# A mixture-of-experts decoder layer on one core: one pair of experts combined per turn, single buffers, four more weight tiles filled early, six PSUM banks in one rotation, and the last down weights in a half and two quarters

## The chip, the core and the metric

The kernel runs on one core of a Trainium2 chip. It is one program: TensorE (PE) multiplies, VectorE (DVE) and ScalarE (ACT) read the products out of PSUM, GpSimd (POOL) fetches rows of tokens by index, and SyncE (SP) issues the transfers of the weights from HBM, which the core's 16 DMA engines carry out. The metric is the device time of one execution in microseconds (us). Three runs of the kernel before took 767.46, 767.82 and 767.86 us, with a median of 767.82 us.

## The reference: what is computed

One decoder layer on 512 tokens of width 1024. The first part is a shared norm, an input projection, a short gated convolution, differential attention and an output projection. The second part is a mixture of 32 experts (4 groups of 8): each token picks the best group and its two best experts in it.

```python
hn2 = rms_norm(h, ffn_norm_g[l]).reshape(Bsz * S, D)
# hierarchical_moe, S = 512 tokens, D = 1024, D_EXPERT = 512:
p_group = softmax(hn2 @ w_router_group);  g_idx = argmax(p_group);  g_gate = max(p_group)
logits_sel = (hn2 @ w_router_expert) of the chosen group
top_vals, top_idx = lax.top_k(logits_sel, 2);  top_w = softmax(top_vals)
comb = onehot(g_idx) * (sum of onehot(top_idx) * top_w) * g_gate
for g in range(G):
    hg = jnp.einsum('td,edf->tef', h, w_gate[g])
    hu = jnp.einsum('td,edf->tef', h, w_up[g])
    act = jax.nn.silu(hg) * hu * comb[:, g, :, None]
    y = y + jnp.einsum('tef,efd->td', act, w_down[g])
```

All inputs are float32. Each expert has three matrices of 2 MB (gate, up, down), so the 32 experts hold 192 MB of weights, and every one of them is read once.

## The kernel before

The first part (to line 650) runs projection, convolution, attention and the first half of the output projection. From line 692 the second half of the output projection, the router and the places of the tokens in the experts are computed (lines 840 to 862).

The second part takes the experts in 16 pairs. Each expert has 64 slots for tokens, so a pair fills 128 partitions. A weight matrix is cut into pieces of 1 MB: four pieces for gate and up of an expert, two for down, 192 pieces in all. The list `pieces` (lines 703 to 709) is the order in which SP issues them: gate and up of expert 2q, the four down pieces of pair q-1, gate and up of expert 2q+1. A piece goes into a tile; there are 17 of them, the 16 tiles of `ring` (named `we`) and one tile `wm` in the pool `moe` (line 728). Before the router twelve pieces are issued (`pump(RING - 4)`, line 737), after it five more (line 866), because the last four tiles of `ring` and the space of `moe` are still used by the first part. From there `used(n)` (line 1119) counts tiles that PE has read, and SP issues one new piece into each.

A turn q of the loop at line 1146 does, in this order on PE:
- `expert(2q)`: gate and up (`gate_up`, lines 966 and 967, tile `pgu`), two matmuls side by side in the two halves of the array. ACT applies silu into its own tile `sil` (line 972) and DVE multiplies into `act` (line 973).
- `down_t(q-1)`: the activations of the pair before are transposed (`pat2`, line 979) and copied to SBUF by ACT (`aT`, line 981).
- `turned(q+1)`: the rows of the next pair (`xr`) are transposed (`pxt2`, line 953) and scaled into `xt` by ACT (line 959) and DVE (line 956).
- `down_pair(q-1)`: the down matmuls (`pdn`, line 990), whose result is split into a rounded part `rh` (ACT, line 1007) and a rest `rl` (DVE, line 1008). `sel` (line 1018) holds a one for each token and slot that belong together.
- `expert(2q+1)`.
- In even turns the indices and the rows of two pairs are made ready (`prepare`, lines 934 to 944; POOL fetches `xr` at line 925 and the gates `cw` at line 930), and `combine_all` adds two pairs into the output `y`: eight times four matmuls into one bank (`pcb`, lines 1026 and 1027) and one addition by DVE (line 1030).

The tiles `xr`, `xt`, `act`, `rh`, `rl` and `sel` have two buffers each. The eight PSUM banks are two each for `G` (pgu), `A` (pat2, pxt2, pi), `D` (pdn) and `C` (pcb), at line 1111.

After the loop (lines 1164 to 1176) pair 14 is combined, the activations of pair 15 are transposed, its down matmuls run in two halves of 512 columns (`down_cols`, line 999), each half is split and combined, and the output leaves in eight transfers (line 1175). `overflow` (line 1054) reads a count (`tot`) into a register of each engine and loops over experts with more than 64 tokens; the count itself is computed by DVE in turn 1 (`overflow_count`, lines 1035 to 1047).

The order on each engine is the order of the code (`manual_schedule`); the waits between engines are put in from the tiles that they share.

Of the kernel before, what the change touches and what calls it, by code (L numbers as in the profile page):

```python
# [17 lines left out]
P = 128  # L18
D = 1024
S = 512  # L20
# [12 lines left out]
MORE = 1  # L33
# [6 lines left out]
def layer(ctx: ExitStack, tc: tile.TileContext, x, attn_norm_g, w_in, conv_w, conv_out_g,  # L40
# [653 lines left out]
    ws_cm.__exit__(None, None, None)  # L694
    kp = ctx.enter_context(tc.tile_pool(name="kp", bufs=1, side="right", reuse_waits="tile"))
# [17 lines left out]
    def w_src(e, j):  # L713
# [6 lines left out]
        if isinstance(e, int) and e >= NE - 2:  # L720
            return src[:, :, 512 * (j - 4):512 * (j - 4) + 512], (4, 512)
        return src[:, 2 * (j - 4):2 * (j - 4) + 2], (2, 1024)

    def load_piece(e, j):
        src, shape = w_src(e, j)
        i = slot[0] % (RING + MORE)
        slot[0] += 1
        t = rtile("we", [P, *shape]) if i < RING else moe.tile([P, *shape], F32, name="wm", tag=f"wm{i}")
        nc.sync.dma_start(t, src)
        return t  # L730
# [6 lines left out]
    pump(RING - 4)  # L737
# [157 lines left out]
    HS = (slice(0, SLOTS), slice(SLOTS, P))  # L895
    vcol = kp.tile([P, PAIRS], F32, name="vcol")
    tokrow = kp.tile([P, S], F32, name="tokrow")
# [20 lines left out]
    def fetch(i, m):  # L918
        x = moe.tile([P, D], F32, name="xr", tag="xr", bufs=2)
# [14 lines left out]
    def prepare(qs, tag="A"):  # L934

        n = len(qs)
        oh = one_hot(posm[:, :, 2 * qs[0]:2 * qs[0] + 2 * n], 2 * n)

        def rest():
            ix = [index(oh[:, :, P * j:P * (j + 1)], vcol[:, q:q + 1], tag) for j, q in enumerate(qs)]  # L940
            for q, i in zip(qs, ix):
                rows[q], cws[q] = fetch(i, P)
            return lambda: [fetch_gates(cws[q], i, P) for q, i in zip(qs, ix)]
        return rest

    def turned(x, m, tag="A"):

        xt = moe.tile([P, KD, P], F32, name="xt", tag="xt", bufs=2)
# [260 lines left out]
```

## Time and profile before

| | |
|---|---|
| median of three runs | 767.82 us |
| profiled execution, its own time | 767.56 us |
| its span in the trace | 765.8 us |
| mean granted TensorE clock | 0.975 of full speed |
| busy: PE, PE weight loads, DVE, ACT, POOL | 690.6, 379.6, 300.9, 192.4, 76.4 us |
| moved by DMA | 229.68 MB |
| weights of the experts | 192 transfers of 1024 KB |

The profile's own time is 1.8 us longer than the span, which counts from the first instruction to the last. The busy time of PE holds the modelled ends of pipelined matmuls that overlap, two side by side in the expert part, so it does not say that PE is the limit. Stage by stage the profile has to be read with the share of the DMA engines and the rate beside it: the first 220 us have little DMA, and from about 290 us on to 730 us the DMA engines are busy all the time.

### The profile page before, as it was taken

To read this page: it belongs to the slowest core of one execution; us is meant where nothing else is said; L and a number is where in the kernel's file an instruction comes from. 1 tells how busy PE (TensorE), PEld (TensorE's weight loads), DVE (VectorE), ACT (ScalarE), POOL (GpSimd) and SP (SyncE) were. 2 spreads that over 40 slices of the span, in tenths; PEclk is the share of its full clock that TensorE was granted. 3 is DMA by queue.
4 is the path that set the end of the run, shared out by engine and by line. 5 is a ranking of instruction groups with operands and counts; after the bars stand their busy time and mean duration, and the time that the engine had idled before them with its cause. 6 is when DMAs were issued, how large, how long until landed. Compare 5 with 4: busy or idle time off the path is not lost.

```text
span 765.8 us, 8682 instructions
## 1 busy us (share of the span) xinstructions
PE 690.6 (90%) x3272; PEld 379.6 (50%) x3272; DVE 300.9 (39%) x593; ACT 192.4 (25%) x413; POOL 76.4 (10%) x103
## 2 busy tenths in 40 slices
PE   6998999999899659999999999989989988998984
PEld 5886788777778423334335344334334334333331
DVE  2565866777551722143224134124123223113232
ACT  3555445555341211110211021111010210110100
POOL 5021301121010122002002002002002002000001
PEclk9999999999999859999999999999999999999997
DMA  8221222211159959999999999999999999999942
GB/s 260 85 83 55 83 58 72 64 56 56 56 180 422 384 184 415 417 422 416 421 422 415 422 421 416 422 420 416 422 419 417 422 420 419 419 422 422 408 156 110
DMA packets 54842, 229.68 MB, mean 300 GB/s; under 512 B 6303, under 2 KB 20912, under 8 KB 30736
## 3 DMA queue, kind: packets, MB, share of 16 engines
q1 hardware_dynamic: 50384, 222.32, 72.4%
q0 software_dynamic: 3312, 4.64, 2.0%
q10 hardware_dynamic: 1104, 2.17, 0.7%
q8 instruction: 26, 0.43, 0.2%
q14 instruction: 16, 0.13, 0.0%
HBM read 229.16 MB, written 4.26 MB: 305 GB/s over the span
## 4 chain that ended last, share of the span: by engine, by line
PE 52%; DMA 29%; DVE 9%; ACT 5%; issue 2%; POOL 1%; SPq 0%; DVEq 0%; POOLq 0%; ACTq 0%
DMA we<-in_w_exp_up_dram 18%; PE pgu L966 13%; PE pdn L990 7%; DMA we<-in_w_exp_down_dram 6%; PE pgu L967 4%; DMA wm<-in_w_exp_down_dram 3%; PE pq L118 3%; PE pq L119 3%; PE pq L117 3%; PE pcb L1026 2%; DMA xr<-hrow,idx 2%; PE pcb L1027 2%; PE pcv L117 1%; PE pcv L119 1%; PE pcv L118 1%
## 5 line engine op out<-in xcount | busy, mean ns | idle before, releaser
L967 PE MATMUL pgu<-we,xt 128*64 128x512 f32 x488 | 218.4, 599 | 13.7 <-DMA we<-in_w_exp_up_dram 13.7
L966 PE MATMUL pgu<-we,xt 128*64 128x512 f32 x480 | 215.1, 599 | 0.8 <-ACT xt L959 0.8
L973 DVE SCALAR_TENSOR_TENSOR act<-sil,cw,pgu 64x512 f32<-64x512 f32 x32 | 36.0, 1126 | 222.7 <-ACT sil L972 222.7
L990 PE MATMUL pdn<-we,aT 128*64 128x512 f32 x448 | 109.4, 598 | 0.8 <-ACT aT L981 0.8
L966 PEld LDWEIGHTS pgu<-we,xt 128*64 128x64 f32 x480 | 64.4, 138 | 90.3 <-issue 85.9
L967 PEld LDWEIGHTS pgu<-we,xt 128*64 128x64 f32 x488 | 65.3, 138 | 64.2 <-issue 37.2
L972 ACT ACTIVATE sil<-pgu,cw 64x512 f32<-64x512 f32 x32 | 21.9, 683 | 289.5 <-PE pgu L967 264.7
L990 PEld LDWEIGHTS pdn<-we,aT 128*64 128x64 f32 x448 | 35.1, 138 | 58.9 <-issue 54.5
L1026 PE MATMUL pcb<-rh,sel 128*128 128x512 f32 x128 | 55.1, 430 | 9.0 <-DVE y L1030 9.0
L1008 DVE TENSOR_TENSOR rl<-pdn,rh 128x512 fp32r<-128x512 f32 x32 | 22.1, 692 | 89.9 <-ACT rh L1007 89.9
L1030 DVE TENSOR_TENSOR y<-y,pcb 128x512 f32<-128x512 f32 x70 | 47.1, 687 | 21.8 <-PE pcb L1027 21.5
L1027 PE MATMUL pcb<-rl,sel 128*128 128x512 f32 x128 | 51.1, 400 | 0.6 <-DVE rl L1008 0.6
L925 POOL DMA_INDIRECT xr<-hrow,idx x16 | 16.1, 1004 | 344.3 <-DVE vcol L915 332.5
L109 DVE TENSOR_TENSOR wlo<-raw,whi 128x1024 fp32r<-128x1024 f32 x30 | 37.7, 1255 | 22.7 <-ACT whi L102 22.7
L1007 ACT ACTIVATE rh<-pdn 128x512 fp32r<-128x512 f32 x32 | 19.1, 597 | 100.4 <-PE pdn L990 96.6
L117 PE MATMUL pq<-whi,xh 128*128 128x512 f32 x96 | 40.9, 427 | 2.5 <-DVE st0h L356 1.6
L117 PE MATMUL pcv<-xh,whi 128*128 128x512 f32 x96 | 41.8, 435 | 0.0
L118 PE MATMUL pq<-wlo,xh 128*128 128x512 f32 x96 | 38.9, 405 | 0.5 <-DVE wlo L109 0.5
L119 PE MATMUL pq<-whi,xl 128*128 128x512 f32 x96 | 39.1, 407 | 0.0
L119 PE MATMUL pcv<-xh,wlo 128*128 128x512 f32 x96 | 38.1, 397 | 0.0
L1026 PEld LDWEIGHTS pcb<-rh,sel 128*128 128x128 f32 x128 | 24.4, 191 | 27.5 <-DVE y L1030 20.3
L118 PE MATMUL pcv<-xl,whi 128*128 128x512 f32 x96 | 37.9, 395 | 0.0
(233 smaller groups left out, 923.5 us busy)
## 6 DMA issues: line engine op xcount, KB each, us to landing
we<-in_w_exp_up_dram SPq DMA_DIRECT2D x61, 1024.0 KB, 19.8
we<-in_w_exp_gate_dram SPq DMA_DIRECT2D x60, 1024.0 KB, 19.8
we<-in_w_exp_down_dram SPq DMA_DIRECT2D x60, 1024.0 KB, 19.8
raw<-in_w_in_dram SPq DMA_DIRECT2D x24, 512.0 KB, 3.7
raw<-in_w_out_dram SPq DMA_DIRECT2D x8, 512.0 KB, 3.9
wm<-in_w_exp_gate_dram SPq DMA_DIRECT2D x4, 1024.0 KB, 19.8
wm<-in_w_exp_down_dram SPq DMA_DIRECT2D x4, 1024.0 KB, 19.8
wm<-in_w_exp_up_dram SPq DMA_DIRECT2D x3, 1024.0 KB, 19.8
```

The source lines that it names most:

```text
L109: V.tensor_sub(los[i], raws.pop(i), his[i].bitcast(F32))
L117: T.matmul(o, lh, rh, start=start, stop=False)
L118: T.matmul(o, lh, rl, start=False, stop=False)
L119: T.matmul(o, ll, rh, start=False, stop=stop)
L966: T.matmul(p[HS[1 - h]], l, w[2 * (k // 4)][:, k % 4], start=(k == 0), stop=(k == KD - 1))
L967: T.matmul(p[HS[h]], l, w[2 * (k // 4) + 1][:, k % 4], start=(k == 0), stop=(k == KD - 1))
L973: V.scalar_tensor_tensor(act[HS[h]].rearrange("s (c q) -> s q c", c=4), t[HS[h]].rearrange("s (q c) -> s q c", c=4), w, p[HS[h]].rearrange ...
L990: T.matmul(p[hf][HS[h]], aT[:, c, HS[h]], ws2[h][c // 2][:, c % 2, hf * 512:(hf + 1) * 512], start=(c == 0), stop=(c == 3))
L1008: V.tensor_sub(r[1][0:m, hf], p[0:m], r[0][0:m, hf].bitcast(F32))
L1026: T.matmul(p, s[0:m, ts], rh[0:m, hf], start=(n == 0), stop=False)
L1027: T.matmul(p, s[0:m, ts], rl[0:m, hf], start=False, stop=(n == last))
L1030: V.tensor_add(ys, ys, p)
```

## The change

The pieces are issued in the same order, except that in the last turn expert 31 comes ahead of the down pieces of pair 14. The pool `wm` has four tiles of its own, made as soon as the pool `ws` of the first part is closed; pieces 12 to 15 go there, and 16 pieces are issued before the router instead of twelve. There are 20 tiles in all instead of 17. `xr`, `xt`, `act`, `rh`, `rl` and `sel` have one buffer each, `sil` is gone (silu is written into `act` and multiplied in place), and `act` is written in its natural order and read with a stride by the transposes. One pair is prepared and one pair is combined in each turn, with two matmuls per bank. `turned` moves to the end of the turn. PSUM is `G` with two banks and `X` with six. The count of overflowing experts is read into registers in turn 1 (`more`). The last down matmuls run over 512, 256 and 256 columns; a tile holds a quarter of both experts.

```diff
-MORE = 1
+MORE = 4
+EARLY = RING - 4
...
     ws_cm.__exit__(None, None, None)
+    wm = ctx.enter_context(tc.tile_pool(name="wm", bufs=MORE, side="right", reuse_waits="tile"))
...
     for q in range(PAIRS):
         pieces += [(2 * q, j) for j in range(4)]
-        if q:
-            pieces += [(2 * q - 2 + h, 4 + j) for j in range(2) for h in range(2)]
-        pieces += [(2 * q + 1, j) for j in range(4)]
-    pieces += [(NE - 2 + h, 4 + j) for j in range(2) for h in range(2)]
+        downs = [(2 * q - 2 + h, 4 + j) for j in range(2) for h in range(2)] if q else []
+        second = [(2 * q + 1, j) for j in range(4)]
+        pieces += second + downs if q == PAIRS - 1 else downs + second
+    pieces += [(NE - 2, 4), (NE - 1, 4), (NE - 2, 5), (NE - 2, 6)]
...
+        if EARLY <= i < EARLY + MORE:
+            t = wm.tile([P, *shape], F32, name="wm", tag="wm")
+        else:
+            t = rtile("we", [P, *shape])
+        if two:
+            for h in range(2):
+                nc.sync.dma_start(t[:, h], quarter(e + h, j))
...
-    pump(RING - 4)
+    pump(EARLY + MORE)
...
-        t = moe.tile([P, FE], F32, name="sil", tag="sil")
-        A.activation(t[HS[h]], p[HS[1 - h]], AF.Silu, scale=r)
-        V.scalar_tensor_tensor(act[HS[h]].rearrange("s (c q) -> s q c", c=4), t[HS[h]].rearrange("s (q c) -> s q c", c=4),
-                               w, p[HS[h]].rearrange("s (q c) -> s q c", c=4), op0=OP.mult, op1=OP.mult)
+        a = act[HS[h]]
+        A.activation(a, p[HS[1 - h]], AF.Silu, scale=r)
+        V.scalar_tensor_tensor(a, a, w, p[HS[h]], op0=OP.mult, op1=OP.mult)
...
-    def combine(parts, m, c, hf, to=None):
-        p = bank("C", "pcb")
+    def combine(s, rh, rl, m, c, cs, to=None):
+        p = bank("X", "pcb", (P, cs.stop - cs.start))
...
-    ready = [prepare((q,), "S")() for q in range(2)]
+    ready = [prepare(0, "S")()]
+    rest = prepare(1, "S")
     gates()
     xts = {0: turned(rows.pop(0), P, "K")}
+    ready.append(rest())
...
-    BANKS = {"G": 2, "A": 2, "D": 2, "C": 2}
+    BANKS = {"G": 2, "X": 6}
...
     for q in range(PAIRS):
         expert(2 * q)
         if q:
             aT = down_t(acts.pop(q - 1), P)
-        if q + 1 < PAIRS:
-            xts[q + 1] = turned(rows.pop(q + 1), P)
...
+        if q == LAST:
+            expert(2 * q + 1)
         if q:
             down_pair(q - 1, aT)
-        expert(2 * q + 1)
+        if q < LAST:
+            expert(2 * q + 1)
+            xts[q + 1] = turned(rows.pop(q + 1), P)
+        if q + 2 < PAIRS:
+            rest()()
         if q == 1:
             inc = overflow_count()
-        if more:
-            rest()()
-        if q and q % 2 == 0:
-            combine_all((q - 2, q - 1))
+            more = nc.values_load(tot[0:1, 0:1], min_val=0, max_val=NE)
+        if 0 < q < LAST:
+            combine_all(q - 1)
...
+    def last_combine(n):
+        cs = cols[n]
+        for c in range(NT):
+            combine(sel, *r, P, c, cs, yt[:, n % 2, 0:cs.stop - cs.start] if c == 1 else None)
+            nc.sync.dma_start(oc[:, c, cs], y[:, c, cs])
+
+    last_down(0)
+    last_down(1)
+    last_combine(0)
+    last_down(2)
+    last_combine(1)
+    last_combine(2)
```

On ACT, in the middle of the loop of the kernel before, two turns stand like this (`sil` is silu, `aT` the copy of the transposed activations, `xt` the scaled rows of the next pair, `rh` the rounded part of the down result):

```order
210 L972 ACTIVATE sil<-pgu,cw 64x512 x2
211 L981 ACTIVATE aT_3294<-pat_3289 128x512
212 L959 ACTIVATE xt<-pxt_3297,gf 128x128 x4
213 L1007 ACTIVATE rh<-pdn 128x512 x2
214 L972 ACTIVATE sil<-pgu,cw 64x512 x2
```

In the changed kernel the same place of ACT's queue holds one whole turn (here silu has the name `act`):

```order
215 L985 ACTIVATE act<-pgu,cw 64x512
216 L994 ACTIVATE aT_3324<-pat_3319 128x512
217 L1020 ACTIVATE rh<-pdn 128x512 x2
218 L985 ACTIVATE act<-pgu,cw 64x512
219 L972 ACTIVATE xt<-pxt_3390,gf 128x128 x4
220 L985 ACTIVATE act<-pgu,cw 64x512
```

The scaling of the next pair's rows has moved from the middle of the turn, ahead of the split, to its end, behind the silu of the pair's second expert.

On DVE the end of the kernel before, from the last product of an activation on, is this (`y` is the addition into the output, `rl` the rest of the split, `sel` the ones):

```order
481 L973 SCALAR_TENSOR_TENSOR act<-sil,cw,pgu 64x128x4
482 L1018 TENSOR_SCALAR sel<-tokrow,vcol 128x512
483 L1030 TENSOR_TENSOR y<-y,pcb 128x512 x8
484 L1008 TENSOR_TENSOR rl<-pdn,rh 128x512
485 L1030 TENSOR_TENSOR y<-y,pcb 128x512 x3
486 L1008 TENSOR_TENSOR rl<-pdn,rh 128x512
487 L1030 TENSOR_TENSOR y<-y,pcb 128x512 x3
488 L1056 TENSOR_LOAD tot
```

In the changed kernel the end of DVE's queue, from the same product on, is this:

```order
499 L986 SCALAR_TENSOR_TENSOR act<-act,cw,pgu 64x512 x2
500 L1031 TENSOR_SCALAR sel<-tokrow,vcol 128x512
501 L1021 TENSOR_TENSOR rl<-pdn,rh 128x512 x2
502 L1041 TENSOR_TENSOR y<-y,pcb 128x512 x8
503 L1031 TENSOR_SCALAR sel<-tokrow,vcol 128x512
504 L1021 TENSOR_TENSOR rl<-pdn,rh 128x512
505 L1021 TENSOR_TENSOR rl<-pdn,rh 128x256
506 L1041 TENSOR_TENSOR y<-y,pcb 128x512 x3
507 L1021 TENSOR_TENSOR rl<-pdn,rh 128x256
508 L1041 TENSOR_TENSOR y<-y,pcb 128x256 x6
```

Both experts of the last pair are now finished ahead of the split of pair 14, and the last half is cut into two quarters whose additions come last.

On SP, this is what stands around the pieces 9 to 17 of the kernel before (`we` is a tile of the ring, `wm` the tile beside it):

```order
21 L729 DMA we<-in_w_exp_up_dram 128x2048
22 L729 DMA we<-in_w_exp_gate_dram 128x2048
23 L729 DMA we<-in_w_exp_up_dram 128x2048
24 L729 DMA we<-in_w_exp_down_dram 128x2048 x4
25 L729 DMA wm<-in_w_exp_gate_dram 128x2048
26 L729 DMA we<-in_w_exp_up_dram 128x2048
```

In the changed kernel the same pieces stand like this:

```order
21 L743 DMA we<-in_w_exp_up_dram 128x2048
22 L743 DMA we<-in_w_exp_gate_dram 128x2048
23 L743 DMA we<-in_w_exp_up_dram 128x2048
24 L743 DMA wm<-in_w_exp_down_dram 128x2048 x4
25 L743 DMA we<-in_w_exp_gate_dram 128x2048
26 L743 DMA we<-in_w_exp_up_dram 128x2048
```

The four down pieces of pair 0 go to the four separate tiles, and the four pieces behind them to the last four tiles of the ring.

## Rows read from the trace of the kernel before

**Rows 1.** The page's second part: 40 slices of the span, 19.1 us each.
```profile
PE   6998999999899659999999999989989988998984
DMA  8221222211159959999999999999999999999942
GB/s 260 85 83 55 83 58 72 64 56 56 56 180 422 384 184 415 417 422 416 421 422 415 422 421 416 422 420 416 422 419 417 422 420 419 419 422 422 408 156 110
```
**Rows 2.** Busy us by stretch: PE, PEld, DVE, ACT, POOL, then clock, DMA share, GB/s.
```profile
275.00:287.00 12.00, 9.24 (x38) 4.51 (x40) 0.79 (x2) 1.14 (x4) 2.00 (x2) 0.64 0.20 45
...
490.00:698.00 208.00, 188.49 (x862) 78.62 (x858) 53.78 (x81) 29.07 (x63) 11.98 (x12) 1.00 1.01 420
698.00:737.00 39.00, 35.41 (x154) 15.02 (x154) 12.41 (x18) 3.85 (x6) 0.00 (x0) 1.00 0.96 388
```
**Rows 3.** SP's instructions in order of time, 255 to 286 us: start, length.
```profile
255.34 10.28 SPq L729 DMA_DIRECT2D we<-in_w_exp_down_dram  x4
265.79 0.80 SPq L729 DMA_DIRECT2D wm<-in_w_exp_gate_dram  x1
285.33 0.33 SPq L729 DMA_DIRECT2D we<-in_w_exp_up_dram  x1
```
**Rows 4.** The chain that ended last, 268 to 310 us: start, length, what.
```profile
270.97 5.84 DMA xr<-hrow,idx
...
288.75 1.10 PE pxt L953 x8
...
299.24 8.53 DMA xr<-hrow,idx
```
**Rows 5.** The same chain: one place of the turn, two turns apart.
```profile
331.21 0.69 ACT sil L972
...
386.34 0.69 ACT sil L972
...
441.46 0.69 ACT sil L972
```
**Rows 6.** Instructions in order of time, 695 to 720 us; in brackets idle time and releaser.
```profile
698.08 0.64 PE L967 MATMUL pgu<-we,xt 128*64 128x512 f32 x1 [1.33 <-DMA we<-in_w_exp_up_dram]
...
710.42 0.64 PE L966 MATMUL pgu<-we,xt 128*64 128x512 f32 x1
...
717.44 0.65 PE L979 MATMUL pat<-idf,act 128*128 128x128 f32 x4
...
718.30 0.60 ACT L981 ACTIVATE aT<-pat 128x512 f32<-128x512 f32 x1
...
718.95 7.09 PE L990 MATMUL pdn<-we,aT 128*64 128x512 f32 x32 [0.85 <-ACT aT L981]
```
**Rows 7.** DVE in order of time: first and last step of the overflow count.
```profile
326.19 0.18 DVE L1036 TENSOR_SCALAR nt<-cnt 128x32 f32<-128x32 f32 x1
...
329.43 0.15 DVE L1045 CAST tot<-inc 128x1 int32<-128x1 f32 x1
```
**Rows 8.** The chain that ended last, 700 to 766 us.
```profile
705.14 0.23 PE pcb L1026
...
732.95 0.69 ACT sil L972
733.66 1.11 DVE act L973
...
739.21 0.43 PE pcb L1027
...
742.57 7.09 PE pdn L999 x32
```
**Rows 9.** The last additions into the output, in order of time.
```profile
755.87 1.28 DVE L1030 TENSOR_TENSOR y<-y,pcb 128x512 f32<-128x512 f32 x2 [0.82 <-PE pcb L1027]
```
**Rows 10.** Groups of instructions: line, engine, count, busy us, mean ns, idle before.
```profile
L1008 DVE TENSOR_TENSOR rl<-pdn,rh 128x512 fp32r<-128x512 f32 x32 | 22.1, 692 | 89.9 <-ACT rh L1007 89.9
L1030 DVE TENSOR_TENSOR y<-y,pcb 128x512 f32<-128x512 f32 x70 | 47.1, 687 | 21.8 <-PE pcb L1027 21.5
...
L1007 ACT ACTIVATE rh<-pdn 128x512 fp32r<-128x512 f32 x32 | 19.1, 597 | 100.4 <-PE pdn L990 96.6
```

More of the change, by code (lines that the diff above doesn't have):

```diff
@@ L932, in fetch_gates, with prepare, turned @@
                              bounds_check=S - 1, oob_is_err=False)
-    def prepare(qs, tag="A"):
-        n = len(qs)
-        oh = one_hot(posm[:, :, 2 * qs[0]:2 * qs[0] + 2 * n], 2 * n)
+    def prepare(q, tag="X"):
+        oh = one_hot(posm[:, :, 2 * q:2 * q + 2], 2)
         def rest():
[L940 to L943, printed above, removed]
-        return rest
-    def turned(x, m, tag="A"):
-        xt = moe.tile([P, KD, P], F32, name="xt", tag="xt", bufs=2)
+            i = index(oh, vcol[:, q:q + 1], tag)
+            rows[q], cws[q] = fetch(i, P)
+            return lambda: fetch_gates(cws[q], i, P)
+        return rest
+    def turned(x, m, tag="X"):
+        xt = moe.tile([P, KD, P], F32, name="xt", tag="xt")
         x = x.rearrange("s (q k) -> s k q", k=KD)
@@ L984, in down @@
     def down(ws2, aT):
-        p = [bank("D", "pdn") for _ in range(2)]
+        p = [bank("X", "pdn") for _ in range(2)]
         for c in range(4):
@@ L1087, in overflow @@
             gate_up(w, xt, 0, p)
-            act = moe.tile([P, FE], F32, name="act", tag="act", bufs=2)
+            act = moe.tile([P, FE], F32, name="act", tag="act")
             activate(act, p, 0, cw[0:SLOTS, NE:NE + 1], wcol[0:SLOTS])
@@ L1127, in expert @@
         if not h:
-            acts[q] = moe.tile([P, FE], F32, name="act", tag="act", bufs=2)
+            acts[q] = moe.tile([P, FE], F32, name="act", tag="act")
         p = bank("G", "pgu")
@@ L1137, in down_pair, with combine_all @@
         parts[q] = (select(vcol[:, q:q + 1], P), *down_split(p, P))
-    def combine_all(qs):
+    def combine_all(q):
         for c in range(NT):
-            for hf in range(2):
-                combine([parts[q] for q in qs], P, c, hf)
-        for q in qs:
-            parts.pop(q)
+            for cs in HALF:
+                combine(*parts[q], P, c, cs)
+        parts.pop(q)
+    LAST = PAIRS - 1
     for q in range(PAIRS):
@@ L1158, in layer @@
+        if q + 2 < PAIRS:
+            rest()()
         if q == 1:
             inc = overflow_count()
-        if more:
-            rest()()
-        if q and q % 2 == 0:
-            combine_all((q - 2, q - 1))
-    q = PAIRS - 1
-    sel = select(vcol[:, q:q + 1], P)
-    combine_all((q - 1,))
-    aT = down_t(acts.pop(q), P)
-    r = split_tiles()
-    yt = moe.tile([P, 2, 512], F32, name="yt", tag="xr", bufs=2)
-    pd = [down_cols([wt.pop((2 * q + h, 4 + hf)) for h in range(2)], aT) for hf in range(2)]
@@ new lines, in layer, with last_down @@
+    r = split_tiles()
+    yt = moe.tile([P, 2, 512], F32, name="yt", tag="xr")
+    e = 2 * LAST
+    cols = (slice(0, 512), slice(512, 768), slice(768, D))
+    def last_down(n):
+        if n == 0:
+            w = [wt.pop((e + h, 4)) for h in range(2)]
+        else:
+            w = wt.pop((e, 4 + n))
+            w = [w[:, h] for h in range(2)]
+        p = down_cols(w, aT)
+        split_cols(r, p, cols[n], P)
+    def last_combine(n):
[3 more added lines that the diff above has]
+            nc.sync.dma_start(oc[:, c, cs], y[:, c, cs])
```

73 lines of the change are left out of this document (36 added, 37 removed).

## The prediction

> **What bounds the kernel now.** I read the slices of the page first. PE is busy at nine tenths nearly everywhere, but in the expert part two matmuls run side by side and their modelled ends overlap, so the row that counts is the DMA row beside it: from slice 16 on it is at nine tenths and the rate stays at 415 to 422 GB/s until slice 37 [rows 1]. By stretches, the DMA share is 1.01 at 420 GB/s from 490 to 698 us, and 0.20 at 45 GB/s in the 12 us from 275 to 287 [rows 2]. That hole is the first thing to see: SP's queue has sent its seventeenth piece at 265.8 us and can send no other before PE has read the first tile, at 285.3 us [rows 3]. What PE waits for there is the fetch of pair 0's rows, which took 5.84 us [rows 4].
>
> The second thing is who waits for whom in the loop. At first PE is behind, since it starts with 17 full tiles: two turns take 55.1 us, 331.21 to 386.34 to 441.46 [rows 5]. DMA needs more. Of the 192 pieces, 17 are in before the hole and 16 come after the piece for which PE waits at 698.08 us [rows 6], so 159 pieces took 698.1 - 287 = 411 us, 2.585 us each with the fetched rows among them, 31.0 us for a turn of twelve. PE catches up, and at 698.08 us it waits 1.33 us for a weight.
>
> The third thing is the end. Behind 698.08 us no DMA wait stands in the way any more; the last addition into the output ends at 755.87 + 1.28 = 757.15 us [rows 9], 59.1 us later, and the span ends 8.65 us after that. So three terms decide: the hole, whether PE's new turn is still shorter than DMA's, and the length of the end.
>
> **The hole.** Three more tiles hold three more pieces. A piece is 1.049 MB, at 420 GB/s 2.50 us, so 7.5 us of transfers move into a hole of about 11 us. The tiles must be free in time: pieces 12 to 15 no longer wait for the ring (255.3 to 265.6 us in [rows 3]), and the four behind them take over those waits. Against this stands PE's start. The fetch of pair 0's rows ran partly into an idle DMA; the next one, 28 us later beside full queues, took 8.53 us [rows 4]. So the start moves by 0 to 2.7 us, and the first free tile with it. I take 1.5 us, between the two rows, and a gain of 6.0 us (4.8 to 7.5). DMA's restart goes from 287 to 288.5 us with three pieces fewer left; the piece of 698.08 us lands at 692.1.
>
> **PE's turn.** From the start of a gate-up group: 7.02 us to the transposes (710.42 to 717.44), 0.65 for these [rows 6]. Silu now writes into `act`, so it has to wait for the transposes that read it; before, it ran beside them. Then 0.69 for silu [rows 8], 0.60 for the copy `aT` [rows 6] and 0.1 for the hand-overs: the down matmuls start at 9.06 us, where the row of before gives 718.95 - 710.42 = 8.53. They last 7.09 [rows 6], to 16.15. The second gate-up takes 732.95 - 726.04 = 6.9 [rows 6, 8], to 23.1. The transposes of the next rows take 1.10 [rows 4], now at the turn's end; the index matmuls and changes of bank 0.3 (an estimate, from what is left of 55.1 when its other groups are taken away); the combine 16 matmuls of 0.23 [rows 8] = 3.7. Sum: 28.2 us.
>
> What hides the new waits there: with one `xt`, ACT and DVE may scale only behind the second gate-up, and do so while PE runs the combine. Silu and four scalings end 0.69 + 1.15 us behind it, DVE's product and its half 1.11 + 0.69 us behind silu's end; the fourth and fifth `pcb` want the banks of `pxt2` back, and PE comes to them 2.8 us behind the group. The additions by DVE, now eight in every turn instead of in every other, are 8 x 0.687 = 5.5 us [rows 10], longer than PE's 3.7, but six banks let PE run ahead and the rest lies beside the next gate-up. The single `xr` is fetched at a turn's end and read 23 us into the next. The strided transposes and the contiguous product I take at 0; bounds -0.5 and +0.5 a turn, from the product's 1.11. If PE's cover were gone, a turn would cost 2 us more, and rival four prices that.
>
> Turn 1 is special: PE, like the others, loads the count into a register ahead of the combine, and DVE computes it behind the product and its scaling. The count takes 3.4 us [rows 7]; with the load PE waits about 5.5 us, once. SP waits too, but it has nothing to send before the next gate-up.
>
> Timeline of PE: gate-up of expert 0 ends at 288.75 + 1.5 = 290.2, expert 1's at 297.2, turn 1 starts at 299.0 when `xt` is there, turn 2 at 299.0 + 28.2 + 5.4 = 332.6. At that time DMA has 20 + (332.6 - 288.5) / 2.585 = 37 pieces in, three under its bound of 40, so the count's wait does not stop it. Turn 14 starts at 332.6 + 12 x 28.2 = 671.0, and PE wants the piece of 692.1 at 671.0 + 16.15 + 3.5 = 690.6. So DMA still decides, by 1.5 us; with 3.4 us of waits in what follows (next part) the turn may be 28.6 us before anything is lost.
>
> **The end, counted from that piece (692.1).** PE finishes the gate-up (3.5), the transposes, the combine (3.7) and expert 30 by 15.5. Expert 31 follows, its last piece landing as the eighth at 20, and ends at 23.4. The down pieces of pair 14 land up to 30, the twelfth times 2.5; their second half of matmuls ends at 33.4. Without any wait for pieces PE would be there at 30.0: that is the 3.4 us. Then rounding and rest of both halves, 0.60 + 0.69 + 0.69 = 2.0 [rows 10], and eight additions of 0.69: 41. PE is through its combine at 38.5, the activations of pair 15 are ready, so half 0 of the last down ends at 42.0 (half of 7.09 [rows 8]), the first quarter at 43.8. The quarter has no row: between half and all of 3.5 us, I take half, as the columns are. Combine of the half to 46.0, second quarter to 47.8, its split about 1.0 (less than 0.60 + 0.69), combine about 1, and six additions of 256 columns at about 0.4 (an estimate, 0.35 to 0.69): 51.4 us. Before it was 59.1, so 7.7 us go: before, combine, transposes and the whole down group stood one behind the other, and at 739 us PE's steps were 0.43 instead of 0.23 us [rows 8], after 3 us of waiting for silu, product and addition. What is late next is the second quarter's split and its additions. The four further output transfers lie beside the additions except the last, as before. The register load on SP ran while the last transfer was on its way: 0, at best -0.5. Bounds of the term: -4 (steps of 0.43 us in a combine again, and full-length quarters) and -9.
>
> **Sum.** Span 765.8 - 6.0 - 7.7 = 752.1; the execution's own time is 1.8 us more (767.56 against 765.8): 753.9. The median of the runs is 0.26 above the profiled execution, so 754.0 is what I predict, 13.8 us or 1.8% less than 767.82.
>
> **Rivals.**
> 1. PE becomes the limit. For it: only 0.4 us a turn are left between 28.2 and 28.6, and every buffer that had a second copy now adds a hand-over. Against it: the groups are taken from rows that contain hand-overs. At 29.0 us a turn it costs 12 x 0.4 = 5 us: 759.
> 2. The hole is not filled: the rows for pair 0 arrive much later because more transfers are queued ahead of them. For it the 8.53 us, against it that DMA was full during most of the 5.84 too. With 4 us more instead of 1.5 the gain is 3.5, with 6 it is 1.5: 758.
> 3. The end shrinks less, since PE's clock falls: the granted clock there was 0.5 at the steps of 0.43 us, that is 1.2 instead of 2.4 GHz. For it: PE waits between 33.4 and 34.7 and again for the quarters. Against it: the wait before the fall was 3 us. Price 8 x 0.46 = 3.7 us: 757.5.
> 4. Slower than before: the single buffers put the scaling chain of `xt` bare into each turn, because the combine waits for the same banks that the scaling must give back. Then PE stands for 0.69 + 1.15 us and a hand-over, 2 us, in each turn: 30.2 us, 12 x 1.6 = 19 us, 773. It beats the gains from a turn of 28.6 + 13.8 / 12 = 29.8 us on. For it: six banks serve four uses. Against it: the first three `pcb` need only banks that ACT and DVE left 7 us earlier.
>
> The Trainium skill ("Trainium Kernel Development and Optimization", Best Practices) asks for double buffers so that transfers overlap compute, which speaks for rivals 1 and 4: by that rule the fetch of 8.53 us would stand open in each turn with one `xr`, and 12 x (28.2 + 8.5 - 28.6) = 97 us would be added. The rows speak against so much, since 8.53 us is far under the 23 us between issue and use; I give that version 1 in 100, inside rival 4.
>
> **How the numbers follow.** Forecast 0.60, rival 1 0.19, rival 2 0.09, rival 3 0.07, rival 4 0.05. The forecast's own range is 751 to 757 (6.0 with its 4.8 to 7.5, 7.7 with about 1.5 either way). Taking in rivals 1 to 3 it becomes 750.5 to 760. Faster by over 0.2% (1.5 us, about what a measurement of this kernel tells from no change) is all but rival 4 and a small part of rival 1 at 30 us a turn: 0.93; same 0.02; slower 0.05.
>
> **What would show it.** Right: a DMA share near 1 up to about 283 us and again from 288; one wait of PE for the count near 325 us; turns of 28 us on PE at first and waits of PE for weights again in the last turns; the last piece for expert 29 near 692 us and 51 us from there to the last addition. Wrong: idle DMA engines in turns 1 to 3, no DMA wait of PE at the end (rival 1 or 4), a fetch of pair 0's rows over 9 us (rival 2), a clock of 0.5 behind the last down group (rival 3).

## The result and the profile after

The changed kernel takes 756.45 us (median of four runs, 755.12 to 757.1), the kernel before on the same chip 767.64: a ratio of 0.9856 with a 95% interval of 0.9837 to 0.9875. A second set of runs of the same file gave 755.6 us, 0.9851 (0.9836 to 0.9867). The prediction was 754.0 us: right in sign and near in size, 11.2 us where 13.8 were expected.

Executions differ by up to 1.3 us in the first part, so the table counts from a fixed point, the issue of the first expert weight.

| from the trace, us | before | after | after, again |
|---|---|---|---|
| first weight issued at | 222.39 | 221.27 | 222.50 |
| from there to expert 0's first matmul | 57.42 | 60.07 | 60.08 |
| from there to the piece of expert 29 for which PE waits | 475.69 | 471.67 | 471.45 |
| from that piece to the end of the last addition | 59.07 | 50.41 | 50.35 |
| from there to the end of the span | 8.65 | 9.95 | 10.0 |

So the piece comes 4.0 us earlier, the end is 8.7 us shorter, and the output after it 1.3 us longer: 4.0 + 8.7 - 1.3 = 11.4 us.

The slices of the page, to be read beside [rows 1]:

```profile
PE   6998999999899829979999999999999999998984
DMA  8221211222139998999999999999999999999973
GB/s 264 87 84 57 85 57 57 68 62 67 57 123 423 383 401 312 417 419 415 417 419 421 417 419 422 418 419 421 417 417 422 417 420 422 417 420 420 420 281 113
```

Counted from 0, slice 14 moves 401 GB/s where it moved 184; in slice 15 a hole stays (312). The windows (busy time and instructions of the five engines, then clock, DMA share, GB/s), the first and the last two against [rows 2]:

```profile
275.00:287.00 12.00, 7.82 (x36) 4.05 (x38) 0.92 (x4) 1.14 (x4) 3.02 (x3) 0.60 0.67 252
275.00:281.00 6.00, 2.16 (x16) 2.01 (x16) 0.68 (x3) 1.14 (x4) 0.00 (x0) 0.50 1.02 418
326.00:334.00 8.00, 6.28 (x18) 4.75 (x20) 5.28 (x15) 0.00 (x0) 0.13 (x1) 0.60 1.01 415
490.00:692.00 202.00, 191.35 (x914) 80.20 (x910) 66.77 (x120) 30.56 (x64) 13.94 (x14) 1.00 1.01 419
692.00:737.00 45.00, 41.69 (x192) 18.57 (x193) 15.58 (x26) 6.56 (x13) 0.00 (x0) 1.00 0.85 338
```

The hole's share rose from 0.20 to 0.67. The loop is as full as before, 419 against 420 GB/s. SP's queue and the chain of waits show why the hole did not close (against [rows 3, 4]):

```profile
254.25 10.05 SPq L743 DMA_DIRECT2D wm<-in_w_exp_down_dram  x4
...
286.62 0.33 SPq L743 DMA_DIRECT2D we<-in_w_exp_gate_dram  x1
```

```profile
269.51 8.70 DMA xr<-hrow,idx
...
281.34 1.08 PE pgu L979
...
327.02 0.70 issue
...
328.49 0.43 PE pcb L1038
...
368.80 0.69 PE pat L992 x4
...
396.74 0.69 PE pat L992 x4
```

The three further pieces go out at 268.5 to 269.8 us, just ahead of the fetch of pair 0's rows or with it. That fetch took 8.70 us instead of 5.84, so PE and the first free tile are late. Two turns' transposes are 27.94 us apart. PE's waits from 280 to 700 us (us in total, times, longest) hold 1.4 us a turn for the copy `aT`, one wait for the count and one for a weight (a second one, 0.45 us, is in the rows after these):

```profile
PE pdn L1003 <- ACT aT L994: 19.6, 14, 1.4
PE pcb L1037 <- DVE it L1057: 5.3, 1, 5.3
PE pgu L980 <- DMA wm<-in_w_exp_up_dram: 1.3, 1, 1.3
```

The last turns and the end in order of time, against [rows 6, 9]; idle time and releaser in brackets (`pat` are the transposes of the activations, once a turn):

```profile
620.40 0.75 PE L992 MATMUL pat<-idf,act 128*128 128x128 f32 x4
...
648.39 0.75 PE L992 MATMUL pat<-idf,act 128*128 128x128 f32 x4
662.36 0.64 PE L980 MATMUL pgu<-we,xt 128*64 128x512 f32 x1 [0.45 <-DMA we<-in_w_exp_up_dram]
...
677.85 0.75 PE L992 MATMUL pat<-idf,act 128*128 128x128 f32 x4
...
692.94 0.64 PE L980 MATMUL pgu<-wm,xt 128*64 128x512 f32 x1 [1.33 <-DMA wm<-in_w_exp_up_dram]
...
708.25 0.75 PE L992 MATMUL pat<-idf,act 128*128 128x128 f32 x4
...
715.85 0.59 PE L1003 MATMUL pdn<-we,aT 128*64 128x512 f32 x1
...
717.81 3.65 PE L1003 MATMUL pdn<-we,aT 128*64 128x512 f32 x16 [0.93 <-DMA we<-in_w_exp_down_dram]
722.86 3.65 PE L1003 MATMUL pdn<-we,aT 128*64 128x512 f32 x14 [1.40 <-DMA we<-in_w_exp_down_dram]
726.44 0.75 PE L992 MATMUL pat<-idf,act 128*128 128x128 f32 x4
...
738.01 8.71 SPq L1199 DMA_DIRECT2D out_dram<-y  x12
...
741.22 2.07 DVE L1041 TENSOR_TENSOR y<-y,pcb 128x256 f32<-128x256 f32 x6
...
742.62 0.73 POOL L1044 TENSOR_TENSOR y<-y,yt 128x256 f32<-128x256 f32 x1 [0.30 <-ACTq L1067]
```

Turns are 27.99 us long until 648.39, then 29.46 and 30.40: there PE waits for weights, 1.5 + 2.4 = 3.9 us in all (the brackets show only part of it). The down group of pair 14 takes 10.6 us (715.85 to 726.44) where it needs 7.0, so 3.6 us more. These 7.5 us are PE's room (6.6 in the second execution). Before, no weight held PE up behind 698.08 us. The last addition ends at 743.35 us, and SP's last issue at 746.72.

### The profile page after: what moved, and what is told of

It reads as the page before. It is cut to its first block, busy times and chain, and to the rows that moved or that the text cites. A ratio compares the mean times of both kernels' runs of the same rounds, so it can differ in the third digit from the quotient of the medians.

```text
span 753.3 us, 8889 instructions
## 1 busy us (share of the span) xinstructions
PE 679.5 (90%) x3296; PEld 380.1 (50%) x3296; DVE 318.1 (42%) x660; ACT 194.2 (26%) x415; POOL 75.6 (10%) x103
## 4 chain that ended last, share of the span: by engine, by line
PE 64%; DMA 18%; DVE 8%; ACT 5%; POOL 2%; issue 2%; SPq 0%; POOLq 0%; ACTq 0%
PE pgu L979 20%; PE pdn L1003 11%; DMA we<-in_w_exp_down_dram 8%; DMA we<-in_w_exp_up_dram 5%; PE pcb L1037 3%; PE pcb L1038 3%; PE pq L119 3%; PE pq L118 3%; PE pq L120 3%; DMA wm<-in_w_exp_up_dram 3%; PE pxt L966 2%; PE pcv L118 1%; PE pcv L120 1%; PE pcv L119 1%; DVE wlo L110 1%
## 5 line engine op out<-in xcount | busy, mean ns | idle before, releaser
L979 PE MATMUL pgu<-we,xt 128*64 128x512 f32 x416 | 185.2, 598 | 0.9 <-ACT xt L972 0.8
L980 PE MATMUL pgu<-we,xt 128*64 128x512 f32 x416 | 185.3, 598 | 0.4 <-DMA we<-in_w_exp_up_dram 0.4
L986 DVE SCALAR_TENSOR_TENSOR act<-act,cw,pgu 64x512 f32<-64x512 f32 x32 | 23.9, 746 | 208.9 <-ACT act L985 208.9
L1003 PE MATMUL pdn<-we,aT 128*64 128x512 f32 x384 | 86.3, 595 | 17.7 <-ACT aT L994 15.4
L985 ACT ACTIVATE act<-pgu,cw 64x512 f32<-64x512 f32 x32 | 21.8, 683 | 278.5 <-PE pat L992 164.8
L1041 DVE TENSOR_TENSOR y<-y,pcb 128x512 f32<-128x512 f32 (+1 forms) x129 | 77.4, 669 | 2.8 <-PE pcb L1038 2.6
L1021 DVE TENSOR_TENSOR rl<-pdn,rh 128x512 fp32r<-128x512 f32 (+1 forms) x33 | 22.3, 676 | 97.2 <-ACT rh L1020 95.4
L1037 PE MATMUL pcb<-rh,sel 128*128 128x512 f32 (+1 forms) x132 | 53.3, 406 | 5.3 <-DVE it L1057 5.3
L1038 PE MATMUL pcb<-rl,sel 128*128 128x512 f32 (+1 forms) x132 | 51.7, 393 | 0.0
L1020 ACT ACTIVATE rh<-pdn 128x512 fp32r<-128x512 f32 (+1 forms) x33 | 19.3, 585 | 111.6 <-PE pdn L1003 101.4
L980 PE MATMUL pgu<-wm,xt 128*64 128x512 f32 x96 | 42.6, 595 | 1.4 <-DMA wm<-in_w_exp_up_dram 1.3
L979 PE MATMUL pgu<-wm,xt 128*64 128x512 f32 x96 | 42.8, 595 | 0.0
```

What stands on the lines that cost most here:

```text
L979: T.matmul(p[HS[1 - h]], l, w[2 * (k // 4)][:, k % 4], start=(k == 0), stop=(k == KD - 1))
L980: T.matmul(p[HS[h]], l, w[2 * (k // 4) + 1][:, k % 4], start=(k == 0), stop=(k == KD - 1))
L986: V.scalar_tensor_tensor(a, a, w, p[HS[h]], op0=OP.mult, op1=OP.mult)
L1003: T.matmul(p[hf][HS[h]], aT[:, c, HS[h]], ws2[h][c // 2][:, c % 2, hf * 512:(hf + 1) * 512], start=(c == 0), stop=(c == 3))
L1021: V.tensor_sub(r[1][0:m, cs], p[0:m], r[0][0:m, cs].bitcast(F32))
L1037: T.matmul(p, s[0:m, ts], rh[0:m, cs], start=True, stop=False)
```

## The experiments

Each kernel is the changed kernel with the edit shown, where nothing else is said. The reference for each ratio is the kernel before on the same chip.

**The same file again.**

> The changed kernel as it is, beside the others of this call. Both theories: 756 +- 1.5 us. Shift of the piece for which PE waits in expert 29 against before: 4 to 5 us, end counted from it 50 us.

755.6 us, 0.9851 (0.9836 to 0.9867): the column above.

**Three tiles fewer.**

```diff
-MORE = 4
+MORE = 1
```

> The changed kernel with one extra tile instead of four (17 tiles, 13 pieces ahead of the router). Theory A (the three tiles fill the hole, net of a later start of PE): DMA idle again from about 275 to 286 us, PE starts about 2.5 us earlier, time 4 to 5 us longer than the changed kernel, about 761. Theory B (what the tiles bring is their number in the loop, or nothing): 756 to 757, with the end unchanged.

760.65 us, 0.9916 (0.9902 to 0.9929), 5.0 us more than the second set of the changed kernel. One window, and PE's wait for the piece:

```profile
275.00:281.00 6.00, 3.65 (x20) 2.62 (x22) 0.92 (x4) 1.14 (x4) 1.18 (x2) 0.50 0.03 8
```

```profile
697.88 0.64 PE L980 MATMUL pgu<-we,xt 128*64 128x512 f32 x1 [1.32 <-DMA we<-in_w_exp_up_dram]
```

The DMA engines stand still there (0.03, against 1.02 at 418 GB/s in the changed kernel), the fetch is back at 5.90 us, and the piece comes 475.92 us after the first issue, as before the change (475.69). The tiles are the whole gain of the hole: 4.3 us in the trace, 5.0 in the times.

**Three pieces issued behind the fetch.** Pieces 17 to 19 go out on ACT's queue, behind the gates (how the two helpers hand the engine on is not shown).

```diff
-    pump(RING + MORE)
+    pump(RING + 1)
...
     gates()
+    pump(RING + MORE, A)
```

> The three pieces 17 to 19 are issued on ACT's queue behind the fetch of the rows of pair 0, instead of by SP ahead of it. Theory A (the fetch takes 8.70 instead of 5.84 us because these pieces stand ahead of it in the DMA engines): the fetch of pair 0's rows is back at 5.9 to 6.5 us, PE starts 2 to 2.8 us earlier, the first free tile with it, and the piece for which PE waits at 693 us lands as much earlier: 753.0 to 753.8 us, 2 to 2.6 less than the changed kernel. Rival B (the fetch is long for another reason, or what counts is only the number of bytes): no change, 755 to 756.5. Rival C: the pieces come too late for the hole, and the time grows by up to 3 us.

753.91 us, 0.9831 (0.9816 to 0.9845): the fastest version of the study, 1.7 to 2.5 us under the two sets of the changed kernel, though the intervals overlap. Its chain and SP's queue:

```profile
270.36 6.77 DMA xr<-hrow,idx
...
280.26 1.09 PE pgu L979
```

```profile
286.70 0.33 SPq L743 DMA_DIRECT2D we<-in_w_exp_gate_dram  x1
```

The fetch takes 6.77 us, so two thirds of the 2.9 us that it had grown came from the pieces ahead of it (theory A). The rest can lie in the three pieces that go out while it runs, at 273.7 to 275.4 us; in the two later kernels with this order it took 6.4 and 5.7 us. Counted from the first issue PE starts 1.65 us earlier, but the first tile comes free only 0.5 us earlier: 6.4 us after PE's start instead of 5.3, since PE's first steps, 0.82 us each at a granted clock of 0.50, last until 286 us here. More bytes in the hole do the rest (274 instead of 142 GB/s from 281 to 290 us): the piece comes 1.1 us earlier, after 470.5 us, half of what was expected. In the seven executions that load as the changed kernel does, it comes after 471.0 to 471.8 us. So the trace bears out about 1 us of gain, and the rest of the 1.7 to 2.5 us is no more than what medians of the same loading order differ by (754.9 to 756.6, without the one with the old end).

**PE kept busy during the fetch** (on top of the kernel with the late pieces).

```diff
+    warm = bank("T", "warm")
+    for _ in range(16):
+        T.matmul(warm[0:SLOTS], idf[:, 0:SLOTS], wt[0, 0][:, 0], start=True, stop=True)
     xts = {0: turned(rows.pop(0), P, "K")}
```

> On top of e5_late3, 16 matmuls of PE whose result nobody reads stand ahead of the transposes of pair 0's rows, where PE waits 9.2 us for the fetch. Theory A (the hole ends when PE has read the first tile, and PE reads it at half clock): the granted clock is 1.0 when the fetch lands, the first seven steps of expert 0 take 0.43 instead of 0.82 to 0.85 us, the first free tile is issued 2 to 3 us earlier, and the pieces land as much earlier: 751 to 752 us, 2 to 2.7 less than e5_late3, with PE's waits for weights near 692 us still there. Rival B (PE's pace, not the hole, sets the time, or the clock falls again before the fetch lands): under 0.7 us of gain, 753.2 to 754.5.

758.52 us, 0.9896 (0.9881 to 0.991): 4.6 us slower than without (2.5 in the profiled executions), neither theory. PE, SP, and the window from PE's start to the first free tile:

```profile
267.75 15.62 PE L1116 MATMUL warm<-we,idf 128*64 128x512 f32 x32
...
285.56 0.61 PE L979 MATMUL pgu<-we,xt 128*64 128x512 f32 x1 [0.91 <-DVE cnt L1123]
```

```profile
289.21 0.33 SPq L743 DMA_DIRECT2D we<-in_w_exp_gate_dram  x1
```

```profile
285.50:289.20 3.70, 3.64 (x18) 1.61 (x20) 0.00 (x0) 0.00 (x0) 3.02 (x3) 1.00 0.28 78
```

The experiment was sized wrongly: the 16 became 32 instructions of PE and took 15.6 us, so that they, and not the fetch, held PE until 283.4 us. In its second half it still says something: PE starts 5.3 us later than in the kernel with the late pieces, but at full clock (1.00), and frees the first tile after 3.65 instead of 6.44 us. The half clock costs 2.8 us there; a filler that ends with the fetch was not tried.

**The register load back at the end.**

```diff
-            more = nc.values_load(tot[0:1, 0:1], min_val=0, max_val=NE)
...
-    overflow(inc, more)
+    overflow(inc, nc.values_load(tot[0:1, 0:1], min_val=0, max_val=NE))
```

> The count is read into registers behind the last turn, as in the kernel before, instead of in turn 1. Theory A (DMA sets the pace of the loop, PE has slack in turns 1 and 2): PE's wait of 5.3 us for the count and the half clock behind it go, turn 1 becomes 28 to 30 us instead of 35.7, but the piece for which PE waits lands at the same time, 692 to 694 us; the register load is paid at the end or lies beside the last transfer: time within 1 us of the changed kernel (755 to 757). Rival B (the loop waits for PE): the whole 5 to 7 us of turn 1 come off, 749 to 751 us. Beside it: if the long issue of the last output transfers (1.0 to 1.5 us, 0.33 to 0.40 in the kernel before) comes from where the registers are read, it is gone here, and the span ends 8.7 us after the last addition instead of 9.95.

755.82 us, 0.9856 (0.9839 to 0.9873): no change, theory A. PE is 3.1 us ahead behind turn 2 (transposes at 365.69 instead of 368.80 us), less than the 5.3 us of the wait, because DVE, busy with the count, lets PE stand for a bank for 2.4 us, and the clock is still halved for 3.4 us behind that. So turn 1 takes 32.4 us, not the 28 to 30 that were expected. At 617 us the lead is 3.3 us, at 647 it is 1.7, at 677 it is 0.6: it goes into waits for weights that the changed kernel does not have there, the first of them

```profile
631.17 0.64 PE L980 MATMUL pgu<-we,xt 128*64 128x512 f32 x1 [0.57 <-DMA we<-in_w_exp_up_dram]
```

and the span still ends 10.15 us after the last addition, with one issue of 1.09 us, so the long output is not a matter of where the registers are read.

**One more matmul in each combine.**

```diff
         ts = slice(c * P, (c + 1) * P)
+        T.matmul(p, s[0:m, ts], rh[0:m, cs], start=True, stop=True)
```

> One more matmul (rh with sel, overwritten by the next) in each of a turn's eight combines: 8 x 0.23 = 1.84 us more of PE a turn, nothing else. Theory A (PE's turn of 27.95 us stands 0.4 to 0.6 us under the turn from which PE decides, worked out as 28.6): 27.95 + 1.84 = 29.8 us, 12 to 13 turns, 14 to 17 us more: 769 to 773 us, and PE waits for no weight at 693 us any more. Rival B (DMA has the last word with more slack than that, as the catch-up in 12 turns of 31.0 us of DMA would still be possible): at most 4 us more, 756 to 760 us.

777.83 us, 1.014 (1.0124 to 1.0156): slower than the kernel before. Two turns of its chain:

```profile
432.26 0.69 PE pat L992 x4
...
462.02 0.69 PE pat L992 x4
```

The turn is 29.76 us, as expected, and PE waits for no weight any more. The loss is more than theory A's 14 to 17 us, for two counts that I had wrong. 14 turns have a combine, 14 x 1.84 = 25.8 us; and the room is one sum for the whole loop, 7.5 us, not 0.4 to 0.6 in each turn. Ahead of the last two combines 25.8 - 7.5 = 18.3 us should be lost: the last transposes stand at 744.55 instead of 726.51 us, 18.0 later. The last two combines have the added matmuls too and take 3.1 us more.

**PSUM as before** (the names of the banks change with this line, not shown).

```diff
-    BANKS = {"G": 2, "X": 6}
+    BANKS = {"G": 2, "A": 2, "D": 2, "C": 2}
```

> PSUM as in the kernel before: two banks each for the transposes, the down matmuls and the combine instead of six in one rotation. Theory A (the six banks let PE run ahead of DVE's eight additions of 0.69 us): with two banks PE's combine takes the additions' pace, 8 x 0.69 = 5.5 instead of 3.7 us, a turn 1 to 2 us longer, 29 to 30 us, and 5 to 17 us are lost: 761 to 772 us. Rival B (the wait for the additions is the same either way, or lies beside DMA): 755 to 757 us.

792.39 us, 1.033 (1.0314 to 1.0346): 36 us more, twice theory A's upper end. Its turn, and PE's waits (us in total, times, longest):

```profile
436.51 0.69 PE pat L992 x4
...
467.48 0.69 PE pat L992 x4
```

```profile
PE pi L927 <- ACT xt L972: 11.5, 13, 0.9
PE pcb L1037 <- DVE y L1041: 7.4, 33, 0.3
```

The turn is 30.97 us, 3.0 more. With two banks each the combine goes at the pace of the additions: from its first step to the next gate-up it takes 5.8 us, in the changed kernel 3.8. The other 1.0 is the way from the transposes of the rows to the combine, with 0.9 us a turn of waiting for the scaling of `xt`. The transposes of turn 2 stand 2.8 us later than in the changed kernel, 13 turns add 39, the room takes off 7.5, and the end, where these banks hold up the combine too, is 4.4 us longer: 38.7; the last addition is 37.95 us later. A third of a turn's loss is thus the fourth rival of the prediction, the bare scaling chain, at half of the 2 us that it had priced; it comes true once the six banks are taken away. The larger part is the additions, which the prediction had said that six banks hide.

**More work for PE in turn 14 alone** (the new argument of `combine`, 0 by default, is not shown).

```diff
+        for _ in range(extra):
+            T.matmul(p, s[0:m, ts], rh[0:m, cs], start=True, stop=True)
...
-                combine(*parts[q], P, c, cs)
+                combine(*parts[q], P, c, cs, extra=2 if q == LAST - 2 else 0)
```

> In turn 14 alone each of the eight combines has two more matmuls (rh with sel, overwritten by the next): 16 x 0.23 = 3.7 us more of PE behind expert 29, as much as the second pair cost there in the kernel before. Theory A (from the piece of 692.94 us on PE and the pieces run level: PE waits only 0.93 and 1.40 us for the down pieces of pair 14): those two waits go and 3.7 - 2.3 = 1.4 us are lost, 756.5 to 757.5 us. Rival B (the end is set by PE all through): the whole 3.7, 759 to 760 us. Rival C (by the pieces alone): no change, 755 to 756.2 us.

755.11 us, 0.9842 (0.9829 to 0.9855): no change, rival C. The down group of pair 14 in it:

```profile
720.91 7.04 PE L1003 MATMUL pdn<-we,aT 128*64 128x512 f32 x32
```

It starts 3.7 us later after the piece of expert 29 (26.59 us; 22.91 in the changed kernel), but in one piece: it ends after 33.63 instead of 33.6, and the last addition ends after 50.47 instead of 50.41. So the 3.6 us of room behind the piece are there; theory A had counted only the 2.3 us in the brackets.

**The last turn as before**: expert 31 behind the down pieces of pair 14, the last down in two halves (only the order of the pieces is shown).

```diff
-        pieces += second + downs if q == PAIRS - 1 else downs + second
-    pieces += [(NE - 2, 4), (NE - 1, 4), (NE - 2, 5), (NE - 2, 6)]
+        pieces += downs + second
+    pieces += [(NE - 2 + h, 4 + j) for j in range(2) for h in range(2)]
```

> The changed kernel with the last turn as before: down pieces of pair 14 ahead of expert 31, last down weights in two halves, eight output transfers. Theory A (the end is shorter through the order of the last turn and the quarters): from the last waited piece to the last addition 55 to 58 us instead of 50.4, time 760 to 763. Theory B (the end is shorter only because pair 13 alone, and not two pairs, is combined ahead of expert 30 and no step runs at the lower clock): 51 to 53 us, time 756 to 758.

757.25 us, 0.9878 (0.9863 to 0.9893). The last steps of its chain:

```profile
726.40 0.69 ACT act L985
...
732.33 7.04 PE pdn L1013 x32
```

From the piece (692.80) to the end of the last addition (744.27) it takes 51.5 us, in theory B's range: the place of expert 31 and the quarters are worth 1.1 of the 8.7 us. They are not the whole order of the end. This version keeps the transposes of pair 15 ahead of the combine of pair 14, the split of both halves ahead of the additions of the first, and the contiguous product; in the kernel before all three are otherwise. The other 7.6 can be read against [rows 8, 9]. Expert 31's silu comes 33.6 instead of 34.9 us after the piece. From it to the last down group pass 5.9 us, before 9.6, where PE waited for banks and then stepped at 0.43 us; here each of the 16 steps takes 0.23. From there to the last addition 11.9 instead of 14.6. The last two make 6.3 us; there the six banks, an unbroken clock and that order differ together. The banks alone are worth 4.4 us from the end of pair 14's down group on (the kernel with PSUM as before). Seven steps at 0.43 instead of 0.23 us would be another 1.4 (an estimate, from the steps of the kernel before from 738.4 to 741.2 us). No run takes that order away alone.

**Eight output transfers instead of twelve.**

```diff
-            nc.sync.dma_start(oc[:, c, cs], y[:, c, cs])
+            if n == 0:
+                nc.sync.dma_start(oc[:, c, cs], y[:, c, cs])
+            elif n == 2:
+                nc.sync.dma_start(oc[:, c, HALF[1]], y[:, c, HALF[1]])
```

> The changed kernel with eight output transfers: the two quarters of a block of rows leave together after the second quarter. Theory A (SP issues the twelve transfers too slowly, the last one 2.4 us later than its data): the last issue within 1 us of the last addition, time 1.5 to 2.4 us shorter, about 754.3. Theory B (the late issue was a chance of that execution): no change, 756.4.

756.55 us, 0.9872 (0.9857 to 0.9887): no gain. The span ends 10.6 us after the last addition, and one of the last four issues still takes 1.69 us.

**Two queues for the last quarter.**

```diff
-            nc.sync.dma_start(oc[:, c, cs], y[:, c, cs])
+            (A if n == 2 and c % 2 else nc.sync).dma_start(oc[:, c, cs], y[:, c, cs])
```

> Of the last quarter's four output transfers, those of c = 1 and 3 are issued by ACT instead of SP. Theory A (SP's queue of issues sets the end: its last issue ends 3.4 us after the last addition, four issues of 0.33 to 0.40 us and one of 1.0 to 1.5 among them): SP's last issue ends 0.8 to 2 us earlier, the span ends 8.0 to 9.2 us after the last addition instead of 9.95, and the time is 0.8 to 2 us under the changed kernel: 753.6 to 755. Rival B (what the transfers themselves take decides, rows of 1 KB each): no change, 755 to 756.5.

754.92 us, 0.9847 (0.9835 to 0.986), inside the interval of the changed kernel's second set. The two queues:

```profile
737.34 6.63 SPq L1199 DMA_DIRECT2D out_dram<-y  x10
```

```profile
742.71 0.87 ACTq L1199 DMA_DIRECT2D out_dram<-y  x2
```

The last issue now ends 1.3 us after the last addition (742.68) instead of 3.4, and the span all the same 10.02 us after it: no change, rival B. Theory A, that SP's issues set the end, falls. Rival B's rows of 1 KB are not shown to be the reason: with eight transfers, whose rows have 2 KB, the end is no shorter.

**All together**: the late pieces, the 16 matmuls, the register load at the end and the two queues.

> The 16 matmuls and the late pieces of e9_warm, the register load at the end as in e3_loadend, and the two queues of e8_twoq together. If each gain is what theory A says of it and they add up: 1.7 (late pieces) + 2.3 (clock) + 0 (register load, which only gives PE 3.1 us of slack) + 1.4 (queues) = 5.4 us under the changed kernel: 750.2 us (749 to 751.5). If the two queues bring nothing, 751.5; if the clock brings nothing either, 753.9.

757.0 us, 0.987 (0.9856 to 0.9885): the expectation failed with the 16 matmuls, which again hold PE, until 284.06 us. The piece comes 473.3 us after the first issue, as with them alone (473.45). The version without them was not run, so the fastest that was measured is the one with the late pieces.

## Why the prediction came out nearly right

The sum from the first issue on was to be 6.0 + 7.7 = 13.7 us and was 4.0 + 8.7 - 1.3 = 11.4. The hole gave 2.0 less and the output took 1.3 that the sum did not have; that the end gave 1.0 more than its term, and so covered part of both, is luck. (The prediction's last terms, 753.9 and 0.26, give 754.2 and not 754.0; that changes nothing.)

**The hole: the term that was mis-sized.** The prediction took 1.5 us for PE's later start, "between the two rows" of 5.84 and 8.53 us [rows 4], and a gain of 6.0 (4.8 to 7.5). PE started 2.65 us later, the first tile came free 2.4 (in the second execution 3.1) later, and the gain was 4.0. The fetch is the upper row, not the middle: with the queues full to the end of it nothing of the old conditions was left. That the three pieces do this is shown: it took 8.70 us with all three issued ahead of it, 6.77 with all three issued behind its start, and 5.90 with none of them issued before it had landed. 7.5 - 2.4 = 5.1 leaves 1.1 us unexplained; 419 instead of 420 GB/s over 405 us would be 1.0 of it, which no run tested. In the second execution 7.5 - 3.1 = 4.4 stands against a gain of 4.2, so the rest can also be scatter. Rival 2 was half true: the rows came later because more was queued ahead of them, by 2.9 us where it had asked for 4, and the gain of 4.0 lies between the forecast and its 3.5.

**PE's turn.** 28.2 us forecast, 27.95 measured. The product on DVE, now contiguous, takes 746 ns where it took 1.11 us [rows 8]; the strided transposes take 0.75 where the old ones took 0.65 [rows 6], 0.1 more than the nothing that was assumed. The single `act` costs what was said: PE waits 1.40 us for `aT` instead of 0.85. The additions lie beside the next gate-up as said, and only thanks to the six banks: that is shown by PSUM as before, where the combine takes 2.0 us a turn more.

**DMA or PE?** The prediction gave PE 1.5 us of room up to the piece and 3.4 behind it; measured 3.9 and 3.6 (3.1 and 3.5 in the second execution). That this is one stock for the whole loop is shown from three sides: 25.8 us more of PE in the loop cost 18 there, 3.7 us in turn 14 cost nothing, 3.1 us less gained nothing. Rival 1 stood 7.5 / 13 = 0.6 us a turn away. No turn waits for the single `xr`: PE's only wait for a fetch is the first one, 10.7 us, ahead of turn 0. In the loop 25 us lie between the issue of a fetch (443.4 us) and its use (468.6). So the rule of the Trainium skill ("Trainium Kernel Development and Optimization", Best Practices) to double buffers so that transfers overlap compute does not bind for this fetch, and the 97 us that the prediction worked out from it did not come.

**Turn 1.** The wait for the count was 5.33 us (forecast 5.5). The turn took 35.6 instead of 33.6 us, because behind the wait the granted clock was 0.60 on average from 326 to 334 us and the combine's steps took 0.43. The prediction had not seen this second part. It cost nothing: the later turns, 0.25 us shorter than forecast, gave 3 us back.

**The end.** 51.4 us forecast, 50.4 measured, from 59.1. The second half of pair 14's down group was to end at +33.4 and ends at +33.6; a quarter, which had no row, takes 1.88 us (the second one, alone in the chain), and half of 3.5 had been taken. The prediction's last steps from 47.8 on (1.0, 1 and six times 0.4) add up to 52.2 and not to its 51.4, unless 0.8 of them overlap, which it did not say; measured, 2.9 us pass from the end of the second quarter to the last addition. The clock was 1.00 there, so rival 3 did not come. The prediction gave the gain to the order of the steps in general; the runs give 1.1 of 8.7 us to the place of expert 31 and the quarters, and 4.4 us to the six banks. The rest, with the clock and the other changes of order in it, they do not divide.

**The output.** "Lie beside the additions except the last, as before": this step failed, by 1.3 us. The windows behind the last addition, before and after, part it in two:

```profile
757.16:759.85 2.69, 0.00 (x0) 0.00 (x0) 0.00 (x0) 0.00 (x0) 0.00 (x0) 0.66 0.78 292
759.85:765.79 5.94, 0.00 (x0) 0.00 (x0) 0.00 (x0) 0.00 (x0) 0.00 (x0) 0.50 0.00 0
```

```profile
743.35:747.83 4.48, 0.00 (x0) 0.00 (x0) 0.00 (x0) 0.00 (x0) 0.00 (x0) 0.73 0.61 199
747.83:753.34 5.51, 0.00 (x0) 0.00 (x0) 0.00 (x0) 0.00 (x0) 0.00 (x0) 0.50 0.00 0
```

The transfers go on for 4.5 instead of 2.7 us, and then 5.5 us pass, 5.9 before, in which nothing moves. In all executions with the new loop, the one with the old end too, the first stretch is 3.7 to 4.9 us and the second 5.5 to 6.1. So it is the transfers that end later. One of SP's last issues is long, where the longest had been 0.40 us, and a transfer on one of the queues that fetch instructions (queue, packets, MB, share; from 743.9 to 745.9 us) runs beside it:

```profile
744.23 1.52 SPq L1199 DMA_DIRECT2D out_dram<-y  x1
```

```profile
q8 instruction: 1, 0.02, 3.9%
```

This transfer of 16 KB lands at 745.38 us, 0.37 us ahead of the end of the long issue. In 12 of 13 executions with the new loop SP has an issue of 0.75 to 1.92 us there, and in each of them a transfer of instructions lands 0.35 to 0.48 us ahead of its end. With two queues it starts at 743.90 us, when SP's last issue is all but over, and no issue is above 0.40. In the kernel before the one of 16 KB is through at 745.34 us, ahead of the first output. So SP seems to wait there for its next instructions; no run moved that transfer to test it. It does not set the end alone, since with two queues the output still moves until 4.5 us after the last addition. Fewer transfers and the register load at its old place did not bring the time back either, and why the transfers end later is open.

## What to carry to other kernels

Where two engines race through a long loop, add up the slack of the whole loop, and not of one turn; then a cost per turn is free up to that sum and is paid in full beyond it. Filling an idle stretch of the DMA engines takes away the conditions of whatever small transfer ran there: price that transfer by a row taken beside full queues. A buffer rotation that looks like a detail (six banks instead of three times two) was worth 36 us here, three times the visible change; that it is worth so much because single copies of everything else lean on it is an argument that no run tested.

## What the runs showed of the hardware

The fetch of pair 0's rows by index took 5.84 and 5.90 us where the weights issued ahead of it ran out during it, 5.7 to 6.8 where three more followed it, and 8.6 to 9.1 us where those three stood ahead of it. The granted clock stood at 0.50 (1.2 of 2.4 GHz) in the first steps of expert 0, after PE had waited 7 to 11 us for the fetch, and at 1.00 where the 16 matmuls filled that wait; against that the first tile came free 1.6 us later after PE's start in the changed kernel, and 2.8 with the late pieces. One issue of an output transfer near the end took 0.75 to 1.92 us in 12 of 13 executions with the new loop, each time ending 0.35 to 0.48 us after a transfer of instructions had landed; none took more than 0.40 in the kernel before.
